# Four shared state buffers instead of three in a hybrid decoder layer, with scratch tiles moved between pools

## The chip, the core and the metric

The kernel runs on one core of a Trainium2 chip. The metric is the device time of one execution in microseconds; for the kernel before, the median of three runs is 1130.1 us (1128.6 to 1131.37). A core has five engines that this text names: PE (TensorE, matmuls), DVE (VectorE), ACT (ScalarE), POOL (GpSimd) and SP (SyncE, which here only issues DMAs). Each runs its own instructions in a fixed order and waits on semaphores where it needs another engine's result.

## The reference, cut to what matters

One inference step of a decoder layer. 512 prompt tokens and 8 samples of 8 new tokens each (576 tokens) go through the same weights. The layer has a mixer (a Mamba-2 SSD with 16 heads and an mLSTM with 4 heads, side by side), a cross-attention and a SwiGLU, each in sandwich norms. The change concerns the recurrences of the samples, which start from a given state and return the new one. For every sample:

```python
# SSD, state h of 16 heads x 64 x 128
y_inter = jnp.einsum('btgn,bgjpn->btgjp', cc, h) * jnp.exp(cum)[..., None]
h_new = h * jnp.exp(cum[:, -1])[..., None, None] + jnp.einsum('bsgj,bsgjp,bsgn->bgjpn', to_end, xc, bc)
...
# mLSTM, state c of 4 heads x 128 x 256, with n beside it
num = jnp.einsum('btsh,bshv->bthv', s, vc) + s_inter[..., None] * jnp.einsum('bthd,bhdv->bthv', qc, c_st)
h = num / jnp.maximum(jnp.abs(den), jnp.exp(-m_t))[..., None]
c_new = scale[..., None, None] * c_st + jnp.einsum('bsh,bshd,bshv->bhdv', w_end, kc, vc)
...
h_ml = _rms(h_ml).reshape(bsz, length, ML_INNER) * g_mlstm_out * jax.nn.sigmoid(og)
mix = jnp.concatenate([y_ssd.astype(x.dtype), h_ml.astype(x.dtype)], axis=-1) @ w_out
```

## The kernel before

Activations lie with features on the 128 partitions and the 576 tokens along the free axis. Every weight matrix comes in tiles of 128 x 1024: SP loads `raw` (two buffers), ACT casts the high part `whi`, DVE subtracts to get the low part `wlo` (or POOL issues an accumulating DMA for half of it), three buffers of each, and PE makes three matmuls for each product (high x high, high x low, low x high). `gemm` (lines 201 to 203) does this for all the large projections; the names `ps_in`, `ps_v`, `ps_o` are its PSUM outputs for the input projection, the values and the output projection.

The mixer is written in this order: start and convolutions; gates; the prompt's SSD (`ssd_prompt`); the samples' SSD; q and k (`qk_tile`), v (`gemm_tok`); the prompt's mLSTM, four heads one after the other; the samples' mLSTM in two halves `hb` of four samples; the z and output-gate projections; and the output projection `ps_o`, whose first half needs `mixs_h` and `mixs_l` (the high and low parts of the SSD's result). The order on the chip is another. In this part the framework's scheduler decides at build time: it models the time and puts each engine's instructions into one fixed order, so that the recurrences lie between the matmuls of the projections. Two things bind it. Buffers of one pool and tag are handed out in the order of the program's text, and a tile that takes a used place waits until everything that read the old one is done. That holds too when a pool is closed and another one takes its place, and for the big slots (`SL`).

The samples' SSD holds one tag `t4` of three buffers of 128 x 1024 fp32: `xdts` and `xes` (used first, with the samples' values), and then the states. Step b (0 to 3) loads two states (L711), reads them on PE (`ps_hs`, L715), multiplies them by their decay on POOL (L722), makes two updates each on PE (`ps_hu`, L725), adds these on DVE (L726) and stores the states from the same buffers (L728).

The samples' mLSTM is alike. Its tag `t4` has three buffers for a state of 128 x 4 x 258: load (L909), four reads on PE into `ps_nh` (L911), a masked copy `km` of the keys on ACT (L914, one buffer), four updates `ps_cu` (L918), each added on DVE (L919, which also scales the old state by `es`), store (L921). At the end of each half stand the norm (`head_norm`, L797 and after), the multiplication L933, a transpose on PE (L936) and a copy by ACT into `qk` (L937). `ps_nh`, `ps_cu` and the transpose share two PSUM buffers (`BP`). `head_norm` squares on ACT into a scratch tile `hn_jk` whose contents nobody reads; only the sums go on. The prompt's heads take it from the pool `mp_`, the samples from the pool `ms`.

After both halves L1011 to L1013 merge the samples' part, and `gn_apply` splits the SSD's result into `mixs_h` (ACT) and `mixs_l` (DVE). `mixs_l` lies in slot 2, where `vt4` (the prompt's values) lay, and `mixs_h` in a right-side pool where the samples' tiles lay. L1006 and L1007 split the mLSTM's part, `mixm_h` and `mixm_l`, for the second half of the output projection.

Of the kernel before, what the change touches and what calls it, by code (L numbers as in the profile page):

```python
# [11 lines left out]
F32 = mybir.dt.float32  # L12
F32R = mybir.dt.float32r
BF16 = mybir.dt.bfloat16
# [5 lines left out]
P = 128  # L20
T = 576
# [95 lines left out]
def build(nc, tc, ctx, I, O):  # L117
# [13 lines left out]
    def SL(slot, name, dt=F32, shape=(P, KT, T)):  # L131

        return big.tile(list(shape), dt, name=name, tag="s%d" % slot, bufs=1)
# [26 lines left out]
    def C16(k):  # L160
        a, b = _c16[k]
        return c16[:, a:b]
# [114 lines left out]
    ml = stv.enter_context(tc.tile_pool(name="ml", bufs=1, reuse_waits="tile"))  # L277

    CT = ml.tile([P, 5, 104], F32, name="CT")
    cumst = ml.tile([80, T], BF16, name="cumst")  # L280
    sxst = ml.tile([68, T], BF16, name="sxst")
    mrow = ml.tile([4, TS], F32, name="mrow")
    ncum = ml.tile([P, 4, 16], F32, name="ncum")
    wend = ml.tile([P, 5, 16], F32, name="wend")
    decp = ml.tile([P, 4, 16], F32, name="decp")
    wendm = ml.tile([P, 5, 4], F32, name="wendm")
    scalem = ml.tile([P, 4, 4], F32, name="scalem")
    expnm = ml.tile([P, 4, 4], F32, name="expnm")
# [4 lines left out]
    U, UL = act(uh), act(ul)  # L293
    rxb = ml.tile([P, T], F32, name="rxb")

    wz = ml.tile([P, 256], BF16, name="wz")
    V.memset(wz, 0.0)
    psw = MP("ps_warm")
    for _ in range(NWARM):
# [29 lines left out]
                mm(ps, wl, ah, start=False, stop=k == KT - 1)  # L329
    with tc.issue_after(uhk.ins), tc.issue_after(ulk.ins):  # L330
        w2 = split_w(I["win"][3], cut=1024)
    st = ExitStack()
    sp = st.enter_context(tc.tile_pool(name="startp", bufs=1, reuse_waits="tile"))
    ssqx = sp.tile([P, 640], F32, name="ssqx")
    G.memset(ssqx[:, T:640], 1.0)

# [43 lines left out]
    bcp = stb.enter_context(tc.tile_pool(name="bcp", bufs=1, reuse_waits="tile"))  # L380
    bc = bcp.tile([P, 4, T], F32, name="bc")
    cdup = bcp.tile([16, 2, TS], F32, name="cdup")


    stgp = ExitStack()
# [178 lines left out]
    def ssd_prompt(g):  # L564
        Bt, Ct = bc[:, g, :], bc[:, 2 + g, :]
        ps = MP("ps_bt")
        for c in range(4):
            TE.transpose(ps[:, c * P:(c + 1) * P], Bt[:, c * P:(c + 1) * P], ident)
        btok = sd.tile([P, 4, P], F32, name="btok", tag="btok")
        A.copy(btok, ps.rearrange("p (c k) -> p c k", c=4))  # L570
        ps = MP("ps_cb")
        for c in range(4):
            mm(ps[:, c * P:(c + 1) * P], Bt[:, c * P:(c + 1) * P], Ct[:, c * P:(c + 1) * P], start=True, stop=True,
               skip_group_check=True)
        cbs = sd.tile([P, 512], F32, name="cbs", tag="cbs")
        A.copy(cbs, ps)
        xdt, hs = [], [None]
        for c in range(4):
            ps = MP("ps_xt")
            for j in range(4):  # L580
                TE.transpose(ps[:, j * P:(j + 1) * P], xs[:, g * 4 + j, c * P:(c + 1) * P], ident)
            xd = sd.tile([P, 8, 64], F32, name="xdt", tag="xdt", bufs=4)
            V.tensor_tensor(xd, ps.rearrange("p (h k) -> p h k", h=8),
                            CT[:, c, 32 + 8 * g:40 + 8 * g].unsqueeze(2).to_broadcast([P, 8, 64]), op=ALU.mult)
            xdt.append(xd)
            xe = sd.tile([P, 8, 64], F32, name="xe", tag="xe", bufs=1)
            G.tensor_tensor(xe, xd, wend[:, c, 8 * g:8 * g + 8].unsqueeze(2).to_broadcast([P, 8, 64]), op=ALU.mult)
            ps = MP("ps_h")
            mm(ps, btok[:, c, :], xe.rearrange("p h k -> p (h k)"), start=True, stop=True)
            h = sd.tile([P, 8, 64], F32, name="hs", tag="hs", bufs=4)  # L590
            p3 = ps.rearrange("p (h k) -> p h k", h=8)
            if c == 0:
                V.tensor_copy(h, p3)
            else:
                G.tensor_tensor(h, hs[c], decp[:, c, 8 * g:8 * g + 8].unsqueeze(2).to_broadcast([P, 8, 64]), op=ALU.mult)
                V.tensor_tensor(h, h, p3, op=ALU.add)
            hs.append(h)
        S.dma_start(O["ssmp"][:, g * 512:(g + 1) * 512], hs[4].rearrange("p h k -> p (h k)"))
        for j in range(4):
            jj = g * 4 + j  # L600
            psi = MP("ps_yi")
            lms = []
            for k in range(2):
                h = 2 * jj + k
                psb = MP("ps_l")
                mm(psb, sel[:80, h:h + 1].to_broadcast([80, P]), cumst[:, 0:TP], start=True, stop=True)
                lm = ml.tile([P, 512], F32, name="lm", tag="tmp", bufs=2)
                for c in range(4):
                    V.scalar_tensor_tensor(lm[:, c * P:(c + 1) * P], psb[:, c * P:(c + 1) * P], ncum[:, c, h:h + 1],
                                           C16("maskp"), op0=ALU.add, op1=ALU.add)  # L610
                A.activation(lm, lm, AF.Exp)
                V.tensor_tensor(lm, lm, cbs, op=ALU.mult)
                lms.append(lm)

            for c in range(4):
                for k in (1, 0):
                    mm(psi[64 * k:64 * k + 64, c * P:(c + 1) * P], xdt[c][:, 2 * j + k, :], lms[k][:, c * P:(c + 1) * P],
                       start=True, stop=True, skip_group_check=True)
            pse = MP("ps_ec")
            for k in range(2):  # L620
                mm(pse[64 * k:64 * k + 64, 0:384], sel[:80, 2 * jj + k:2 * jj + k + 1].to_broadcast([80, 64]),
                   cumst[:, P:TP], start=True, stop=True, skip_group_check=True)
            ec = sd.tile([P, 384], F32, name="ec", tag="ec", bufs=1)
            A.activation(ec, pse[:, 0:384], AF.Exp)
            psn = MP("ps_yn")
            for c in range(1, 4):
                mm(psn[:, (c - 1) * P:c * P], hs[c][:, 2 * j:2 * j + 2, :].rearrange("p h k -> p (h k)"),
                   Ct[:, c * P:(c + 1) * P], start=True, stop=True, skip_group_check=True)
            V.tensor_tensor(ec, ec, psn[:, 0:384], op=ALU.mult)
            V.scalar_tensor_tensor(y[:, jj, 0:TP], xs[:, jj, 0:TP], PAR("dskip", jj), psi, op0=ALU.mult, op1=ALU.add)  # L630
            G.tensor_tensor(y[:, jj, P:TP], y[:, jj, P:TP], ec, op=ALU.add)
# [18 lines left out]

    st2 = ExitStack()
    sd = st2.enter_context(tc.tile_pool(name="ssds", bufs=1, side="right", reuse_waits="tile"))
    masks8 = C16("masks")[:TS, :].unsqueeze(1).to_broadcast([TS, 8, TS])
    xdts = sd.tile([TS, 16, 64], F32, name="xdts", tag="t4", bufs=3)
    xes = sd.tile([TS, 16, 64], F32, name="xes", tag="t4", bufs=3)
    btk = sd.tile([TS, 2, P], F32, name="btk")
    for g in range(2):
        ps = BP("ps_xts")
        for j in range(4):
# [11 lines left out]
    for g in range(2):  # L671
        for hb in range(2):
            dst = cpad[:, g, 4 * hb:4 * hb + 4, :].rearrange("p b t -> p (b t)")
            src = bc[:, 2 + g, TP + 32 * hb:TP + 32 * hb + 32]
            for b in range(4):
                G.tensor_copy(dst[:, b * 40:b * 40 + 8], src[:, b * 8:b * 8 + 8])
    decs = sd.tile([P, 16, NB], F32, name="decs")
    psi = BP("ps_yis")
    for g in range(2):
        psb = BP("ps_ls")  # L680
# [25 lines left out]
    psh = BP("ps_hs")  # L706
    hbs = [stacks(sd, btk.rearrange("p g k -> p (g k)"), xes.rearrange("p h k -> p (h k)"), hb, 2) for hb in range(2)]
    for b in range(4):
        hns = [sd.tile([P, 16, 64], F32, name="h0", tag="t4", bufs=3) for _ in range(2)]
        for hb in range(2):  # L710
            S.dma_start(hns[hb], I["h0"][4 * hb + b])  # L711
        for g in range(2):
# [31 lines left out]
        qk_tile(j)  # L744


    vt4 = SL(2, "vt4", F32, (P, 4, 4, 258))
    vt = [vt4[:, c, :, :] for c in range(4)] + [vts]
    for v_ in vt:
        G.memset(v_[:, :, 256:257], 1.0)  # L750
# [45 lines left out]
    def head_norm(num, ex, n4, pool, name):  # L796

        ss = pool.tile([P, n4], F32, name="hn_ss", tag="hn_ss", bufs=2)
        jk = pool.tile([P, 256], F32, name="hn_jk", tag="hn_jk", bufs=1)
        for c in range(n4):  # L800
            A.activation(jk, num[:, c, 0:256], AF.Square, accum_out=ss[:, c:c + 1])
        d = pool.tile([P, n4], F32, name="hn_d", tag="hn_d", bufs=2)
# [71 lines left out]
    for h in range(4):  # L874
        mm(psb[:, h * TS:(h + 1) * TS], sel[:68, h:h + 1].to_broadcast([68, P]), sxst[:, TP:T], start=h == 0, stop=h == 3,
           skip_group_check=True)
    es = ms.tile([P, 4, TS], F32, name="es")
    A.activation(es, pb3, AF.Exp)
    masks4 = C16("masks")[:TS, :].unsqueeze(1).to_broadcast([TS, 4, TS])
    ds_ = ms.tile([TS, 4, TS], F32, name="ds_")  # L880
# [18 lines left out]
    for hb in range(2):  # L899
# [5 lines left out]
               tile_position=(32 * hb, 32 * h), skip_group_check=True)  # L905
        for b in range(4):
            bb = 4 * hb + b
            c0 = ms.tile([P, 4, 258], F32, name="c0", tag="t4", bufs=3)
            S.dma_start(c0, I["c0"][bb])  # L909
            for h in range(4):  # L910
                mm(psn[32 * h:32 * h + 32, 0:257], qpad[:, h, bb, :], c0[:, h, 0:257], start=False, stop=b == 3,  # L911
                   skip_group_check=True)
            km = ms.tile([96, 512], F32R, name="km", tag="km", bufs=1)
            A.activation(km, kst.bitcast(F32), AF.Copy, scale=C32("bmask")[:96, b:b + 1])  # L914
            cn = c0
            for h in range(4):
                ps = BP("ps_cu")
                mm(ps[:, 0:258], km[:, h * P:(h + 1) * P], vst[:, h * 258:(h + 1) * 258], start=True, stop=True)  # L918
                V.scalar_tensor_tensor(cn[:, h, :], c0[:, h, :], es[:, h, 8 * bb + 7:8 * bb + 8], ps[:, 0:258],  # L919
                                       op0=ALU.mult, op1=ALU.add)  # L920
            S.dma_start(O["cs"][bb], cn)  # L921
# [18 lines left out]


    def tmp():
        return ml.tile([P, 512], F32, name="tmp", tag="tmp", bufs=2)

    def z_evac(j):
        def ev(t0, n, ps):
# [36 lines left out]

    mixm_h = SL(3, "mixm_h", F32R)
    mixm_l = SL(4, "mixm_l", F32R)
    ogs = ml.tile([P, KT, TS], F32, name="ogs")

    def og_evac(j):
        def ev(t0, n, ps):
# [1031 lines left out]
```

## Time and profile before

| | |
|---|---|
| median of 3 runs | 1130.1 us (1128.6 to 1131.37) |
| the profiled execution | 1128.78 us, of which the span from first to last instruction is 1127.0 us |
| busy: PE / DVE / ACT / POOL | 1102.2 / 708.2 / 594.3 / 222.5 us |
| mean granted clock of PE | 0.995 |
| HBM read / written | 158.21 MB / 22.22 MB |

The profile is of one execution. "L715" is line 715 of the kernel before. In an answer about waits the columns are: who waited, on what line, for whom; microseconds in total, how many times, the longest. A row that groups instructions has the count (x32), then the busy time in us and the mean duration in ns, then the idle time of the engine just before them. A row of a timeline has start and duration in us. "SPq" rows are the issue of DMAs. PE's matmuls are pipelined: the duration of one is longer than the distance to the next, so distances are taken from starts.

### The profile page before, as it was taken

To read this page: it belongs to the slowest core of one execution; us is meant where nothing else is said; L and a number is where in the kernel's file an instruction comes from. 1 tells how busy PE (TensorE), PEld (TensorE's weight loads), DVE (VectorE), ACT (ScalarE), POOL (GpSimd) and SP (SyncE) were. 2 spreads that over 40 slices of the span, in tenths; PEclk is the share of its full clock that TensorE was granted. 3 is DMA by queue.
4 is the path that set the end of the run, shared out by engine and by line. 5 is a ranking of instruction groups with operands and counts; after the bars stand their busy time and mean duration, and the time that the engine had idled before them with its cause. 6 is when DMAs were issued, how large, how long until landed. Compare 5 with 4: busy or idle time off the path is not lost.

```text
span 1127.0 us, 21146 instructions
## 1 busy us (share of the span) xinstructions
PE 1102.2 (98%) x8423; PEld 1052.4 (93%) x8423; DVE 708.2 (63%) x1401; ACT 594.3 (53%) x1073; POOL 222.5 (20%) x308
## 2 busy tenths in 40 slices
PE   9999999899999999999999999999999999999996
PEld 8999889798998999999988889999999999999996
DVE  6796874457786675668755456667623765447555
ACT  6877533355563365656544445635435674246543
POOL 1333444322122121100134301101001110011001
PEclk9999999999999999999999999999999999999999
DMA  6685565535574447763477855643535774257532
GB/s 211 166 162 128 130 170 162 157 85 142 145 203 108 126 149 267 266 234 100 156 243 280 279 179 174 234 144 95 168 93 118 168 173 124 94 119 169 123 125 85
DMA packets 57127, 181.82 MB, mean 161 GB/s; under 512 B 6300, under 2 KB 10524, under 8 KB 56516
## 3 DMA queue, kind: packets, MB, share of 16 engines
q1 hardware_dynamic: 41732, 137.99, 37.4%
q0 software_dynamic: 15296, 42.47, 18.0%
q8 instruction: 66, 1.08, 0.4%
q14 instruction: 33, 0.27, 0.1%
HBM read 158.21 MB, written 22.22 MB: 160 GB/s over the span
## 4 chain that ended last, share of the span: by engine, by line
PE 81%; DMA 7%; issue 4%; DVE 4%; ACT 3%; SPq 0%; POOL 0%; DVEq 0%; POOLq 0%; ACTq 0%
PE ps_in L201 5%; PE ps_in L203 5%; PE ps_in L202 5%; PE ps_dn L203 4%; PE ps_dn L201 4%; PE ps_dn L202 4%; PE ps_u L1717 3%; PE ps_u L1716 3%; PE ps_u L1715 3%; PE ps_g L1716 2%; PE ps_g L1715 2%; PE ps_g L1717 2%; PE ps_o L203 2%; PE ps_o L201 2%; PE ps_o L202 2%
## 5 line engine op out<-in xcount | busy, mean ns | idle before, releaser
L181 ACT CAST whi<-raw 128x1024 fp32r<-128x1024 f32 x110 | 114.8, 1045 | 102.9 <-PE ps_dn L202 20.0
L201 PE MATMUL ps_in<-uh,whi 128*128 128x320 f32 (+1 forms) x544 | 166.0, 305 | 0.0
L203 PE MATMUL ps_in<-uh,wlo 128*128 128x320 f32 (+1 forms) x544 | 163.2, 300 | 0.5 <-DVE wlo L188 0.5
L202 PE MATMUL ps_in<-ul,whi 128*128 128x320 f32 (+1 forms) x544 | 162.6, 299 | 0.0
L188 DVE TENSOR_TENSOR wlo<-raw,whi 128x1024 fp32r<-128x1024 f32 (+1 forms) x102 | 102.0, 1000 | 74.0 <-ACT whi L181 69.8
L201 PEld LDWEIGHTS ps_in<-uh,whi 128*128 128x128 f32 x544 | 103.5, 190 | 2.7 <-issue 1.2
L203 PEld LDWEIGHTS ps_in<-uh,wlo 128*128 128x128 f32 x544 | 103.4, 190 | 2.4 <-issue 1.3
L202 PEld LDWEIGHTS ps_in<-ul,whi 128*128 128x128 f32 x544 | 103.6, 190 | 0.7
L203 PE MATMUL ps_dn<-hh,wlo 128*128 128x320 f32 (+1 forms) x280 | 82.4, 296 | 0.6 <-DVE wlo L188 0.6
L202 PE MATMUL ps_dn<-hl,whi 128*128 128x320 f32 (+1 forms) x280 | 82.2, 294 | 0.0
L201 PE MATMUL ps_dn<-hh,whi 128*128 128x320 f32 (+1 forms) x280 | 81.9, 295 | 0.0
L203 PEld LDWEIGHTS ps_dn<-hh,wlo 128*128 128x128 f32 x280 | 52.6, 188 | 0.8 <-DVE wlo L188 0.8
L202 PEld LDWEIGHTS ps_dn<-hl,whi 128*128 128x128 f32 x280 | 52.9, 189 | 0.0
L201 PEld LDWEIGHTS ps_dn<-hh,whi 128*128 128x128 f32 x280 | 52.4, 188 | 0.3 <-ACT hh L192 0.3
L186 POOL DMA_DIRECT2D wlo<-win x32 | 28.4, 887 | 94.8 <-ACT wlo L185 84.4
L1715 PE MATMUL ps_g<-b,whi 128*128 128x288 f32 x144 | 42.5, 295 | 0.2 <-ACT cc L1740 0.2
L1716 PE MATMUL ps_u<-b,whi 128*128 128x288 f32 x144 | 42.5, 295 | 0.0
L1716 PE MATMUL ps_g<-b,whi 128*128 128x288 f32 x144 | 42.5, 295 | 0.0
L1715 PE MATMUL ps_u<-b,whi 128*128 128x288 f32 x144 | 42.5, 295 | 0.0
L201 PE MATMUL ps_o<-mixm_h,whi 128*128 128x256 f32 (+1 forms) x128 | 38.8, 303 | 1.5 <-ACT whi L181 1.5
L201 PE MATMUL ps_xo<-qh,whi 128*128 128x288 f32 x128 | 37.8, 300 | 1.0 <-ACT f_xo L1407 1.0
L202 PE MATMUL ps_o<-mixm_l,whi 128*128 128x256 f32 (+1 forms) x128 | 38.5, 302 | 0.0
(722 smaller groups left out, 3654.5 us busy)
## 6 DMA issues: line engine op xcount, KB each, us to landing
raw<-win SPq DMA_DIRECT2D x35, 512.0 KB, 3.7
raw<-wout SPq DMA_DIRECT2D x17, 512.0 KB, 4.3
kva<-kc SPq DMA_DIRECT2D x16, 512.0 KB, 7.2
kva<-vc SPq DMA_DIRECT2D x16, 512.0 KB, 6.3
raw<-wdown SPq DMA_DIRECT2D x16, 512.0 KB, 3.5
raw<-wxq SPq DMA_DIRECT2D x13, 512.0 KB, 3.7
raw<-wgate SPq DMA_DIRECT2D x13, 512.0 KB, 4.1
raw<-wup SPq DMA_DIRECT2D x13, 512.0 KB, 4.7
```

The lines of the kernel that those rows point to most:

```text
L181: A.copy(hi[:, :n], raw[:, :n])
L186: G.dma_start(lo[:, a:b], src[:, a:b], accum_op=ALU.add)
L188: e.tensor_tensor(lo[:, a:b], raw[:, a:b], hi[:, a:b].bitcast(F32), op=ALU.subtract)
L201: mm(ps, wh, ah, start=i == 0, stop=False)
L202: mm(ps, wh, al, start=False, stop=False)
L203: m = mm(ps, wl, ah, start=False, stop=i == len(tiles) - 1)
L1715: mm(ps, wh, b[0][:, k, :], start=start and k == 0, stop=False, skip_group_check=True)
L1716: mm(ps, wh, b[1][:, k, :], start=False, stop=False, skip_group_check=True)
L1717: m = mm(ps, wl, b[0][:, k, :], start=False, stop=k == 3, skip_group_check=True)
```

## The change

Both tags `t4` get four buffers in place of three. To make room, small tiles move:

- `btk`, `decs` (samples' SSD) and `es` (samples' mLSTM) become parts of one slot-2 tile of 4608 columns, `vt4_`, which also holds `vt4` and is now allocated before the samples' SSD;
- `hn_jk` always comes from the pool `mp_`, for the samples too;
- `cumst`, `ncum`, `wend`, `decp` move from `ml` to `bcp`; `lm` (tag `tmp`) to the SSD's pool, `tmp` and `ogs` to `zp`, `wz` to `startp`, which is opened earlier.

No arithmetic is changed.

```diff
-    cumst = ml.tile([80, T], BF16, name="cumst")
-    ncum = ml.tile([P, 4, 16], F32, name="ncum")
-    wend = ml.tile([P, 5, 16], F32, name="wend")
-    decp = ml.tile([P, 4, 16], F32, name="decp")
...
-    wz = ml.tile([P, 256], BF16, name="wz")
+    st = ExitStack()
+    sp = st.enter_context(tc.tile_pool(name="startp", bufs=1, reuse_waits="tile"))
+    wz = sp.tile([P, 256], BF16, name="wz")
...
+    cumst = bcp.tile([80, T], BF16, name="cumst")
+    ncum = bcp.tile([P, 4, 16], F32, name="ncum")
+    wend = bcp.tile([P, 5, 16], F32, name="wend")
+    decp = bcp.tile([P, 4, 16], F32, name="decp")
...
-                lm = ml.tile([P, 512], F32, name="lm", tag="tmp", bufs=2)
+                lm = sd.tile([P, 512], F32, name="lm", tag="tmp", bufs=2)
...
+    vt4_ = SL(2, "vt4", F32, (P, 4608))
-    xdts = sd.tile([TS, 16, 64], F32, name="xdts", tag="t4", bufs=3)
-    xes = sd.tile([TS, 16, 64], F32, name="xes", tag="t4", bufs=3)
-    btk = sd.tile([TS, 2, P], F32, name="btk")
+    xdts = sd.tile([TS, 16, 64], F32, name="xdts", tag="t4", bufs=4)
+    xes = sd.tile([TS, 16, 64], F32, name="xes", tag="t4", bufs=4)
+    btk = vt4_[:TS, 4128:4384].rearrange("p (g k) -> p g k", g=2)
...
-    decs = sd.tile([P, 16, NB], F32, name="decs")
+    decs = vt4_[:, 4384:4512].rearrange("p (h b) -> p h b", h=16)
...
-        hns = [sd.tile([P, 16, 64], F32, name="h0", tag="t4", bufs=3) for _ in range(2)]
+        hns = [sd.tile([P, 16, 64], F32, name="h0", tag="t4", bufs=4) for _ in range(2)]
...
-    vt4 = SL(2, "vt4", F32, (P, 4, 4, 258))
+    vt4 = vt4_[:, 0:4128].rearrange("p (c h k) -> p c h k", c=4, h=4)
...
-        jk = pool.tile([P, 256], F32, name="hn_jk", tag="hn_jk", bufs=1)
+        jk = mp_.tile([P, 256], F32, name="hn_jk", tag="hn_jk", bufs=1)
...
-    es = ms.tile([P, 4, TS], F32, name="es")
+    es = vt4_[:, 4128:4384].rearrange("p (h t) -> p h t", h=4)
...
-            c0 = ms.tile([P, 4, 258], F32, name="c0", tag="t4", bufs=3)
+            c0 = ms.tile([P, 4, 258], F32, name="c0", tag="t4", bufs=4)
...
-        return ml.tile([P, 512], F32, name="tmp", tag="tmp", bufs=2)
+        return zp.tile([P, 512], F32, name="tmp", tag="tmp", bufs=2)
...
-    ogs = ml.tile([P, KT, TS], F32, name="ogs")
+    ogs = zp.tile([P, KT, TS], F32, name="ogs")
```

More of the change, by code (lines that the diff above doesn't have):

```diff
@@ L331, in build @@
         w2 = split_w(I["win"][3], cut=1024)
-    st = ExitStack()
-    sp = st.enter_context(tc.tile_pool(name="startp", bufs=1, reuse_waits="tile"))
     ssqx = sp.tile([P, 640], F32, name="ssqx")
```

## The prediction, made before the changed kernel ran

> **What bounds the kernel now.** First the page of the profile, its busy times and its chain that ended last.
>
> ```profile
> span 1127.0 us, 21146 instructions
> PE 1102.2 (98%) x8423; PEld 1052.4 (93%) x8423; DVE 708.2 (63%) x1401; ACT 594.3 (53%) x1073; POOL 222.5 (20%) x308
> PE 81%; DMA 7%; issue 4%; DVE 4%; ACT 3%; SPq 0%; POOL 0%; DVEq 0%; POOLq 0%; ACTq 0%
> ```
>
> TensorE (PE) is the bound: its matmuls cover 1102.2 of 1127.0 us, and the diff adds and removes none. In the order of the program as built, the changed kernel has the same instructions on every engine, PE's first 1004 matmuls stand as before, and so does everything after the first few output-projection tiles (`ps_o`). So only PE's idle time can change, and only between about 140 us and there, some 405 us. Second view: what PE waited for, of DMAs in that stretch.
>
> ```profile
> PE ps_hs L715 <- DMA h<-h: 2.6, 1, 2.6
> PE ps_nh L911 <- DMA c<-c: 2.0, 1, 2.0
> PE ps_v L774 <- DMA wlo<-wv: 1.1, 2, 0.8
> ```
>
> Two waits are for states (h, c), one each, 2.6 and 2.0 us. Third view: busy times by stretch, in which the column after the engines is the granted clock.
>
> ```profile
> 204.00:208.00 4.00, 2.93 (x24) 2.09 (x25) 0.69 (x1) 0.80 (x2) 1.76 (x1) 1.00 0.40 162
> 360.00:362.00 2.00, 1.50 (x10) 0.69 (x11) 2.00 (x3) 0.27 (x1) 1.19 (x2) 0.65 0.60 162
> 362.00:364.00 2.00, 2.00 (x11) 2.00 (x10) 2.00 (x7) 0.51 (x2) 0.00 (x0) 0.50 0.89 200
> 364.00:372.00 8.00, 8.00 (x63) 8.00 (x63) 3.91 (x10) 3.07 (x5) 0.00 (x0) 1.00 0.19 72
> ```
>
> After the wait for c the clock was granted at 0.65 and 0.50 for two stretches of 2 us: 2 x 0.35 + 2 x 0.50 = 1.7 us of lost matmul time. After the wait for h it stayed at 1.00. [...]
>
> **The change part by part.** *The fourth state buffer, samples' SSD.* The four steps (b = 0 to 3) each load two states, multiply, add, and store from the same buffer; a load into a used buffer waits for the store. These are the links: PE's last update matmul (L725), issue of the store (L728), issue of the next load (L711), and where PE waited.
>
> ```profile
> 158.05 0.47 PE L725 MATMUL ps_hu<-stb,bm 96*128 96x512 f32 x1
> 159.58 0.34 SPq L728 DMA_DIRECT2D o_ssms<-h  x1
> 162.24 0.33 SPq L711 DMA_DIRECT2D h<-h  x1
> 169.66 0.48 PE L725 MATMUL ps_hu<-stb,bm 96*128 96x512 f32 x1
> 171.23 0.34 SPq L728 DMA_DIRECT2D o_ssms<-h  x1
> 176.35 0.33 SPq L711 DMA_DIRECT2D h<-h  x1
> 189.94 1.27 SPq L176 DMA_DIRECT2D raw<-wv  x2
> 190.17 0.39 PE L725 MATMUL ps_hu<-stb,bm 96*128 96x512 f32 x1
> 191.52 0.34 SPq L728 DMA_DIRECT2D o_ssms<-h  x1
> 200.83 0.33 SPq L711 DMA_DIRECT2D h<-h  x1
> 205.07 1.07 PE L715 MATMUL ps_hs<-h,cpad 128*32 128x512 f32 x8 [2.58 <-DMA h<-h]
> DMA to landing us min/median/max: 3.6/4.2/6.4
> ```
>
> With 4.2 us for a landing, the chain from matmul to landed state took 162.24 + 4.2 - 158.05 = 8.4, 176.35 + 4.2 - 169.66 = 10.9, and 14.9 us. The new buffer lets step 1 load early, but the scheduler spends it: as built, step 1's reads stand directly behind step 0's first update, and steps 2 and 3 stand only some 9.6 and 9.9 us of PE work behind the update that their buffer waits for (an estimate, from the matmuls between; before, the one that stalled had 205.07 - 2.58 - 190.17 = 12.3). Such a chain against 9.7 us gives a wait of 0, 1.2 or 5.2 us. The long one had two weight loads issued just ahead of its store (189.94). Two waits of the two shorter kinds give 1.2 together on the mean, two of all three kinds 4.3, against 2.6 saved: -1.4 or +1.7. I take 0 for the net; the ends are -2.6 (no wait) and +7.8 (two long ones). SP's queue meets the same: a load that waits for a store holds the weight loads behind it. The 1.1 us for `wlo` stay: POOL's two multiplies now stand ahead of one weight transfer, where POOL had several us idle.
>
> *The fourth buffer, samples' mLSTM.* The first half's four states load at once, and the second half's four long before their use, so the wait for c and its clock go: -2.0 - 1.7 = -3.7 us. A fourth load in the first burst delays the weight load behind it; cover is the two raw buffers. The second half's stores, on the other hand, come late and stand in SP's queue ahead of the sixth and later output weights; cover: five of these are issued before or between them, and PE needs no sixth for many us after `ps_o` starts.
>
> *The moved tiles.* `wz`, `cumst`, `ncum`, `wend`, `decp`, `lm`, `tmp`, `ogs`, `btk`, `decs`: no instruction more, nothing earlier on PE; `cumst`'s memset goes to a later place of an idle POOL. Zero, the cover being that bc's pool had to be released before the z tiles anyway (`ssqg` lay in its place). `es` now lies in `vt4`'s slot, which `mixs_l` takes next, so `mixs_l` waits for the last samples' update; by the order below it comes behind it in any case.
>
> *The one that matters: `hn_jk`.* This scratch (one buffer) was the samples' own, in `mls`. Now it lies in `mp_`, where the four prompt heads use it; buffers are handed out in program order, and the samples' code stands behind all four heads. So the samples' first norm now waits for the fourth head's squares: in ACT's built order `hn_jk<-nums` directly follows the last `hn_jk<-num`. The first half's transpose (L936) drops behind the last prompt head. The PSUM buffers are handed out in that order too, so the whole second half follows it: 16 reads of states, 16 updates `ps_cu` with 16 additions on DVE, the norm, the transpose. Thirteen of the `ps_cu` stand in one block behind the last `ps_in`, and then come L928, L936 and the first `ps_o`. Before, they were spread between input-projection matmuls. The durations:
>
> ```profile
> L919 DVE SCALAR_TENSOR_TENSOR c<-c,es,ps_cu 128x258 f32<-128x258 f32 x32 | 14.8, 478 | 2.8 <-PE ps_cu L918 2.7
> L1007 DVE SCALAR_TENSOR_TENSOR mixm_l<-qk,ghalf,mixm_h 128x512 fp32r<-128x512 f32 x8 | 5.5, 744 | 0.0
> L914 ACT ACTIVATE km<-sta,c 96x512 fp32r<-96x512 f32 x8 | 5.8, 723 | 5.1 <-PE ps_cu L918 4.9 <-DVE sta L645 0.2
> L188 DVE TENSOR_TENSOR wlo<-raw,whi 128x1024 fp32r<-128x1024 f32 x5 | 6.1, 1222 | 2.0 <-ACT whi L181 2.0
> L994 DVE SCALAR_TENSOR_TENSOR qk<-tmp,qk 128x256 f32<-128x256 f32 x16 | 6.7, 426 | 1.0 <-ACT tmp L992 1.0
> L991 DVE TENSOR_TENSOR tmp<-ps_in,rxb 128x320 f32<-128x320 f32 x8 | 3.9, 491 | 2.8 <-PE ps_in L203 2.7
> ```
>
> And the tail as it ran before, by the timelines of DVE, ACT and PE:
>
> ```profile
> 382.12 0.87 DVE L919 SCALAR_TENSOR_TENSOR c<-c,es,ps_cu 128x258 f32<-128x258 f32 x2
> 394.29 0.15 DVE L812 TENSOR_SCALAR hn_v<-hn_v 128x1 f32<-128x1 f32 x1
> 395.42 0.15 DVE L814 TENSOR_TENSOR hn_a<-hn_y 128x1 f32<-128x1 f32 x1
> 396.19 0.35 DVE L933 TENSOR_SCALAR hns<-nums,hn_a 128x256 f32<-128x256 f32 x1
> 399.19 0.38 PE L936 MATMUL ps_hts<-c,hns 128*128 128x128 f32 x2
> 399.61 0.37 ACT L937 COPY qk<-ps_hts 128x256 f32<-128x256 f32 x1
> 399.88 2.40 ACT L192 CAST mixs_h<-xs 128x576 fp32r<-128x576 f32 x4
> 400.08 0.42 DVE L1011 SCALAR_TENSOR_TENSOR ogs<-ogs,qk 128x256 f32<-128x256 f32 x1
> 400.59 0.76 DVE L193 TENSOR_TENSOR mixs_l<-xs,mixs_h 128x576 fp32r<-128x576 f32 x1
> 408.14 4.72 DVE L1007 SCALAR_TENSOR_TENSOR mixm_l<-qk,ghalf,mixm_h 128x512 fp32r<-128x512 f32 x7
> 404.21 0.31 PE L203 MATMUL ps_in<-uh,wlo 128*128 128x320 f32 x1
> 404.36 0.28 PE L201 MATMUL ps_o<-mixs_h,whi 128*128 128x256 f32 x1
> ```
>
> Before, 5 us of `ps_in` matmuls lay between the last transpose (399.19) and `ps_o` (404.36) and hid the splits of `mixs`. In the built order nothing lies there. From the second half's first `ps_cu`, DVE has in order: 16 L919 at 0.43 (two in 0.87) = 7.0; 8 L1007 at 0.67 (seven in 4.72) = 5.4, whose `mixm_l` nobody needs yet; one L188, 1.1; two L991 and two L994, 1.6; the copy and a small one, 0.5: 15.6 us. Waits inside: some 1.3 us at the second `ps_cu`, which stands behind 24 `ps_in` (0.15 us each, 404.21 to 404.36), and about 1.7 where `km` (one buffer) must be remade on ACT after a step's last `ps_cu` (0.72 and the hand-overs): estimate 3, so 18.6. Then the tail: L928 and its exponential 0.4, five small ones 0.9, POOL's power 1.1 (394.29 to 395.42), 0.8 to L933, 0.5 to the transpose, 0.4 to ACT's copy, 0.5 to L1011, two of these and the first `mixs_l` 1.5: 6.1. With 0.3 to start: 25.0 us. PE's own work over that stretch is 29 `ps_in` (4.4), 15 `ps_cu` (about 0.15 each, 2.3) and the small ones 0.8: 7.5. PE stands for 25.0 - 7.5 = 17.5 us. Bounds: without the inner waits 14.5; with L919 and L1007 at their full 0.478 and 0.744 us and every `km` exposed, 22. Behind it `ps_o` runs on `mixs_l` splits at 0.67 us a piece with L1012 between: +0.7; and the clock falls as behind the wait for c, +1.7 (0 to 3.4, two such stretches).
>
> Sum on the profiled execution, 1128.8 us (span 1127.0): 17.5 + 0.7 + 1.7 - 3.7 + 0 = +16.2, 1145.0. The median of the runs, 1130.1, is 1.3 higher: 1146.3, forecast 1146.
>
> **The rivals.** A, faster: the state waits go and nothing replaces them. [...] It gives 2.6 + 2.0 + 1.7 saved, 1123.8. For it: both waits are in PE's list. It decides if under 7.5 us pass from the second half's first `ps_cu` to the first `mixs_l`; against it, DVE's ordered 15.6 us alone are twice that. 3%.
>
> B, the changed order costs about what the waits gave: a tail stall of 6 us (the second half starting well before PE gets through its `ps_in`), 1130.1 + 6 - 6.3, about 1130. Against it: the second half's matmuls stand behind the transpose. 3%.
>
> C, the tail stall half as long, since DVE's other work finishes before: 9 + 2.4 - 3.7, 1138. 12%.
>
> D, worse: the state chains meet slow stores in both steps (+7.8) and the clock falls there too (+1.7), or a weight load stuck behind a waiting store adds that: 1146 + 9.5, about 1156. 12%.
>
> **How the numbers follow.** My forecast gets 70%: 1146, with its bounds 14.5 to 22 and -2.6 to +4 around it. The range reaches down to C and up nearly to D: 1138 to 1155. A measurement can tell about 0.3% (3.4 us). Faster is A, 3%; same is B, 3%; slower the rest, 94%.
>
> **What would show it.** In the new profile: no wait of PE for c; a stretch around 380 to 405 us where PE idles some 15 us while DVE is full of L919 and L1007, with thirteen `ps_cu` one after the other; `hn_jk<-nums` behind the prompt's squares on ACT; `ps_o` released by `mixs_l`; a granted clock of 0.50 just behind. In the SSD steps waits of `ps_hs` for h of 0 to 5 us. Wrong if `ps_o` starts within 5 us of its place before, or if PE's idle time grew somewhere else.

## The result: slower, 1145.6 us

| | kernel before | changed kernel |
|---|---|---|
| median | 1129.9 us (1128.6 to 1131.4, 4 runs) | 1145.6 us (1143.1 to 1147.8, 4 runs) |
| profiled execution (span) | 1128.8 us (1127.0) | 1145.0 us (1143.2) |

The ratio is 1.0148, with a 95% interval of 1.0122 to 1.0174 (the quotient of the two medians, 1.0139, lies inside it). The forecast was 1146.0, in a range of 1138 to 1155. The medians shift by some 2 us from one series to another, so each kernel below has its ratio to the kernel before in the same series.

The page of the changed kernel, busy times and the chain that ended last:

```profile
span 1143.2 us, 21133 instructions
PE 1109.3 (97%) x8423; PEld 1054.8 (92%) x8423; DVE 708.7 (62%) x1401; ACT 595.2 (52%) x1073; POOL 221.3 (19%) x308
PE 81%; DVE 5%; DMA 5%; issue 4%; ACT 3%; POOL 1%; SPq 0%; DVEq 0%; POOLq 0%; ACTq 0%
```

The span grew by 16.2 us and PE's busy time by 7.1, with the same 8423 matmuls: part of the work ran at a lower clock (on the mean 0.987 after 0.995), as the rows below show. In the chain DMA lost two points and DVE won one. The list of what PE waited for names the place:

```profile
PE ps_cu L919 <- ACT km L915: 5.5, 3, 3.3
PE ps_o L201 <- ACT whi L181: 3.5, 2, 2.1
PE ps_hts L937 <- DVE hns L934: 3.0, 1, 3.0
PE ps_cu L919 <- DVE c L920: 1.9, 4, 0.8
PE ps_o L201 <- ACT mixs_h L192: 1.0, 1, 1.0
```

(Line numbers in that part of the new kernel are one higher.) The waits for h and for c are gone from the list. New are the waits of `ps_cu` for `km` and for the addition on DVE, that of the transpose for `hns`, and the one for `mixs_h`: 5.5 + 3.0 + 1.9 + 1.0 = 11.4 us, all between 398 and 418 us. The busy times by stretch there (PE, weight loads, DVE, ACT, POOL, then the granted clock):

```profile
400.00:404.00 4.00, 1.75 (x4) 1.07 (x4) 4.00 (x8) 4.00 (x7) 0.00 (x0) 0.54 0.75 263
404.00:408.00 4.00, 1.58 (x5) 0.87 (x4) 4.00 (x10) 1.97 (x4) 0.24 (x1) 0.50 0.25 103
...
412.00:416.00 4.00, 0.97 (x4) 0.55 (x4) 1.89 (x11) 0.17 (x1) 2.37 (x6) 0.50 0.42 147
416.00:420.00 4.00, 2.97 (x12) 2.72 (x12) 3.50 (x7) 3.90 (x8) 0.00 (x0) 0.50 0.96 379
420.00:424.00 4.00, 4.00 (x31) 4.00 (x30) 3.82 (x6) 1.73 (x4) 0.00 (x0) 0.90 0.19 68
```

For eight us DVE has no gap, and PE starts eight matmuls (one that runs over 404 us is counted in both rows); ACT is full in the first four. Then follows the tail, in which four engines (PE, ACT, DVE, POOL) hand one small thing to each other (PE 0.97 us of 4). The clock is at half for some 20 us, from about 400 us on (0.54 from 400 to 404, 0.50 from 404 to 420). Two timelines of the same stretch, ACT and PE:

```profile
383.04 0.42 ACT L802 ACTIVATE hn_jk<-num 128x256 f32<-128x256 f32 x1 [2.09 <-DVE num L850]
383.58 0.42 ACT L802 ACTIVATE hn_jk<-nums 128x256 f32<-128x256 f32 x1
...
399.26 1.95 ACT L1007 ACTIVATE mixm_h<-qk,ghalf 128x512 fp32r<-128x512 f32 x3
401.11 0.71 ACT L915 ACTIVATE km<-sta,c 96x512 fp32r<-96x512 f32 x1
401.72 2.55 ACT L1007 ACTIVATE mixm_h<-qk,ghalf 128x512 fp32r<-128x512 f32 x4
```

```profile
392.47 0.38 PE L919 MATMUL ps_cu<-stb,km 96*128 96x258 f32 x1
401.87 0.80 PE L919 MATMUL ps_cu<-stb,km 96*128 96x258 f32 x2 [3.33 <-ACT km L915]
410.61 0.97 PE L919 MATMUL ps_cu<-stb,km 96*128 96x258 f32 x2 [0.36 <-DVE c L920]
417.10 1.06 PE L201 MATMUL ps_o<-mixs_h,whi 128*128 128x256 f32 x3 [1.03 <-ACT mixs_h L192]
417.99 0.58 PE L202 MATMUL ps_o<-mixs_l,whi 128*128 128x256 f32 x1
```

The samples' squares (`hn_jk<-nums`) come directly after the fourth prompt head's (`hn_jk<-num`), as the shared scratch orders it. So the second half's sixteen updates start at 392.47 us, and the last thirteen stand in one block behind `ps_in`. In the kernel before, the last of all 32 updates had started by 385.5 us:

```profile
L918 PE MATMUL ps_cu<-stb,km x32: 279/286/471, 276.7 to 385.5; 96*128 96x258 f32 x32
```

From the second half's first `ps_cu` (392.47) to the first `mixs_l` matmul (417.99) pass 25.5 us. PE is idle for 11.6 us of it. The longest wait, 3.33 us for `km`, is one that ACT caused: it had three splits of `mixm_h` in front of the first copy, and four more in front of the next.

### The profile page after: what moved, and what is told of

It is laid out like the page before. It is cut to its first block, busy times and chain, and to the rows that moved or that the text cites. A ratio compares the mean times of both kernels' runs of the same rounds, so it can differ in the third digit from the quotient of the medians.

```text
span 1143.2 us, 21133 instructions
## 1 busy us (share of the span) xinstructions
PE 1109.3 (97%) x8423; PEld 1054.8 (92%) x8423; DVE 708.7 (62%) x1401; ACT 595.2 (52%) x1073; POOL 221.3 (19%) x308
## 3 DMA queue, kind: packets, MB, share of 16 engines
q0 software_dynamic: 15296, 42.47, 17.8%
## 4 chain that ended last, share of the span: by engine, by line
PE 81%; DVE 5%; DMA 5%; issue 4%; ACT 3%; POOL 1%; SPq 0%; DVEq 0%; POOLq 0%; ACTq 0%
PE ps_in L201 5%; PE ps_in L202 5%; PE ps_in L203 5%; PE ps_dn L203 4%; PE ps_dn L201 4%; PE ps_dn L202 4%; PE ps_u L1718 3%; PE ps_u L1717 3%; PE ps_u L1716 3%; PE ps_g L1716 2%; PE ps_g L1717 2%; PE ps_g L1718 2%; PE ps_o L201 2%; PE ps_o L203 2%; PE ps_o L202 2%
## 5 line engine op out<-in xcount | busy, mean ns | idle before, releaser
L188 DVE TENSOR_TENSOR wlo<-raw,whi 128x1024 fp32r<-128x1024 f32 (+1 forms) x102 | 104.5, 1024 | 86.1 <-ACT whi L181 85.9
L201 PE MATMUL ps_o<-mixs_h,whi 128*128 128x256 f32 (+1 forms) x128 | 38.3, 303 | 1.0 <-ACT mixs_h L192 1.0
```

The costliest lines, as they stand in the source:

```text
L188: e.tensor_tensor(lo[:, a:b], raw[:, a:b], hi[:, a:b].bitcast(F32), op=ALU.subtract)
L201: mm(ps, wh, ah, start=i == 0, stop=False)
```

## The experiments

**The scratch alone, out of the change.** The samples' scratch goes into the slot of their own `hns` tile, which is written only after the squares are used. No space is needed for that.

```diff
-        jk = mp_.tile([P, 256], F32, name="hn_jk", tag="hn_jk", bufs=1)
+        jk = pool.tile([P, 256], F32, name="hn_jk", tag="hn_jk" if n4 > 1 else "hns", bufs=1)
```

> The changed kernel, but the samples' scratch for squares lies in the slot of their own hns tile again (no space more), not in the one that the prompt heads use. Theory (the shared scratch holds the samples' second half back): the sixteen ps_cu spread between ps_in matmuls again, the stall of PE ahead of ps_o (12.7 us of lateness at the first ps_o) and its half clock go, and the gain of the state buffers is left: before minus 3 to 4 us, about 1126 (1124 to 1129). Rival 1 (es in the slot of vt, or another moved tile, holds the output projection back): no change, 1143 to 1147. Rival 2 (the fourth buffers themselves order PE's work badly): 1140 or more.

Measured: 1130.1 us, ratio 1.0017 (0.9997 to 1.0037). The stall is gone: no `ps_cu` is left in PE's list of waits. All moved tiles and the fourth buffers are still there, so neither `es` in the slot of `vt4` nor another moved tile nor the buffers make it by themselves. But the gain that was expected beside that (1126) isn't there. Its waits of PE, and rows of PE and ACT behind the start of the output projection:

```profile
PE ps_o L201 <- ACT whi L181: 3.0, 2, 2.1
PE ps_o L201 <- ACT f_mix L1111: 2.2, 1, 2.2
PE ps_ss L1462 <- DVE ssqxo L1538: 1.9, 1, 1.9
```

```profile
397.50 0.28 PE L201 MATMUL ps_o<-mixs_h,whi 128*128 128x256 f32 x1
403.56 0.41 PE L201 MATMUL ps_o<-mixs_h,whi 128*128 128x320 f32 x1 [2.18 <-ACT f_mix L1111]
```

```profile
398.51 3.78 ACT L1007 ACTIVATE mixm_h<-qk,ghalf 128x512 fp32r<-128x512 f32 x6
402.20 1.04 ACT L868 COPY qk<-ps_ht 128x512 f32<-128x512 f32 x2
403.14 0.37 ACT L1111 COPY f_mix<-ps_o 128x256 f32<-128x256 f32 x1
```

`ps_o` starts at 397.50, 6.9 us before its place in the kernel before (404.36). Then its second group of matmuls waits 2.18 us for the first group's copy, `f_mix`, which stands on ACT behind six splits and two copies of the last prompt head. A matmul that starts at 417.44 in the kernel before starts at 415.44 here, so 2.0 of the 6.9 us are left by then: the wait took 2.2, the granted clock (0.57 from 404 to 408) 4 x 0.43 = 1.7, and the last head's eight transposes, which now stand behind the start of `ps_o` (399.16), the remaining 1.0. The other two waits in the list took 1.5 and 1.9 us more than in the kernel before, and with them the lead is gone.

**The scratch alone, put into the kernel before.** Only that line changes (`pool.tile` to `mp_.tile`).

> The kernel before with one edit: the samples' squares go to the scratch of the prompt heads. Three buffers, es and all small tiles stay. Theory: this edit alone makes the stall; as built, fourteen ps_cu stand in one block ahead of ps_o: plus 17.5 of stall, 2.4 behind it, and minus 3.7 since the samples' late second half no longer waits for c: about 1146 (1142 to 1150). Rivals (moved tiles, buffers): 1130, no change.

Measured: 1154.0 us, ratio 1.0215 (1.0165 to 1.0266). One edit, which changes nothing that is computed, costs at least as much as the whole change (the two intervals just overlap). Its waits of PE:

```profile
PE ps_cu L918 <- ACT km L914: 6.1, 3, 4.4
PE ps_cu L918 <- DVE c L919: 3.3, 5, 1.6
...
PE ps_hs L715 <- DMA h<-h: 2.9, 1, 2.9
PE ps_nh L911 <- DMA c<-c: 2.3, 1, 2.3
```

The direction is as expected, but the time lies above the expected range (1142 to 1150): the size was taken 8 us too low. The -3.7 was wrong: I let the wait for c go with the second half's later place, and it is there. The waits of `ps_cu` are 9.4 us in all, where the changed kernel has 7.4, and the wait for h stays too. The rest of the 8 us was not traced.

**Three buffers in both places, all else as changed.**

> The changed kernel with three buffers in both places again, all tiles moved and the scratch shared. Theory: the stall is there without the fourth buffers: 1143 to 1149, with the wait for h (2.6 us, clock at full speed) back in PE's list. Rival 2 (the fourth buffers order the work badly): back to about 1130.

Measured: 1151.5 us, ratio 1.0208 (1.0166 to 1.0249), 0.6% above the changed kernel and above the expected range (1143 to 1149). So the stall needs no fourth buffer, and rival 2 falls. Its list has the same waits of `ps_cu` as before_shared (6.1 and 3.3 us, the longest 4.4). The wait for h in the list, and the one for c on PE's timeline:

```profile
PE ps_hs L716 <- DMA h<-h: 2.6, 1, 2.6
```

```profile
410.69 1.09 PE L912 MATMUL ps_nh<-c,qpad 128*32 128x257 f32 x8 [2.14 <-DMA c<-c]
```

The wait for c now lies inside the block of `ps_cu`, at half clock (0.50 from 408 to 412). So with the shared scratch the fourth buffers do seem to pay, some 6 us, though the two intervals just overlap: two waits for states (2.6 and 2.1 us), and a shorter block (thirteen `ps_cu` in place of fourteen, with 2.0 us less of waits).

**The splits of `mixm`, held behind the tail.** PE's order up to the start of `ps_o` is the same; ACT and DVE make the eight splits later.

```diff
-    for j in range(8):
-        hm = qk[:, 4 * (j % 2) + j // 2, 0:TP]
+    with tc.issue_after(hts_.ins):
+        for j in range(8):
+            hm = qk[:, 4 * (j % 2) + j // 2, 0:TP]
...
```

(`hts_` is ACT's copy of the samples' last transpose.)

> The changed kernel with the eight prompt splits of mixm (ACT and DVE) held behind the copy of the samples' last transpose; PE's order is the same. Theory (the tail's length is the sum of what DVE and ACT have in order, 5.5 us of it mixm_l and 5 us of ACT's mixm_h ahead of the km): the stretch from the second half's first ps_cu to the first mixs_l matmul shrinks from 25.5 to 20 or 21 us, the time to about 1140.5 (1139 to 1142.5). Rival (the chain ps_cu, addition, next PSUM buffer sets the pace and the splits only fill its gaps): 25 us, 1144 to 1147.

Measured: 1138.8 us, ratio 1.0100 (1.0066 to 1.0134), just below the expected range (1139 to 1142.5); the profiled span is 3.9 us below that of the changed kernel. The wait for `km` in the list, and PE's timeline:

```profile
PE ps_cu L919 <- ACT km L915: 3.2, 3, 1.5
```

```profile
391.90 0.38 PE L919 MATMUL ps_cu<-stb,km 96*128 96x258 f32 x1
402.72 0.80 PE L919 MATMUL ps_cu<-stb,km 96*128 96x258 f32 x2 [0.87 <-ACT km L915]
405.72 0.80 PE L919 MATMUL ps_cu<-stb,km 96*128 96x258 f32 x2 [0.87 <-ACT km L915]
406.88 0.98 PE L919 MATMUL ps_cu<-stb,km 96*128 96x258 f32 x2 [0.36 <-DVE c L920]
413.37 1.06 PE L201 MATMUL ps_o<-mixs_h,whi 128*128 128x256 f32 x3 [1.03 <-ACT mixs_h L192]
414.26 0.58 PE L202 MATMUL ps_o<-mixs_l,whi 128*128 128x256 f32 x1
```

The stretch is 414.26 - 391.90 = 22.4 us, 3.2 shorter, where 4.5 to 5.5 were expected. DVE's 5.5 us of splits were thus a little over half on the path. That the medians lie 6.8 us apart (0.5% by the ratios), more than the stretch or the two profiles show, stays unexplained. With them gone, the chain sets the pace: a step of `km`, four `ps_cu` and four additions takes 3.0 us (402.72 to 405.72), though the four additions are some 1.8 us of it (0.88 us for two, in the changed kernel). Theory and rival both hold a part. From the last pair of `ps_cu` to `ps_o` it is 413.37 - 406.88 = 6.5 us, as in the changed kernel (417.10 - 410.61). In neither kernel does DVE have other work in that tail, so these two do not show what other work there would cost.

**Two buffers of the shared scratch** (and three for c, to make room).

> The changed kernel with two buffers of the shared scratch in place of one, and three buffers for c to make room for it. The samples' first norm then waits for the third prompt head only; as built, six of the second half's sixteen ps_cu stand between ps_in matmuls again and ten stand in one block ahead of ps_o. Theory (the stall is what DVE and ACT have in order from there on): the second half's block is six additions and two km shorter than in three_bufs, so about 6 to 9 us faster than three_bufs (1151.5): 1142 to 1146. Rival (the stall hangs on one wait at the end, whatever stands in the block): as three_bufs, 1149 or more. Other rival (one buffer more frees it all): 1130 to 1133.

Measured: 1145.9 us, ratio 1.0160 (1.0132 to 1.0188). It lies where the theory put it (1142 to 1146), but not for that reason alone. It has four buffers for h, and its list has no wait for h or c (2.6 and 2.1 us in three_bufs); a kernel that differs from it in the scratch alone (one buffer, four for h, three for c) was not run. The waits of `ps_cu` fell only from 9.4 to 7.8 us:

```profile
PE ps_cu L919 <- ACT km L915: 5.8, 2, 4.9
PE ps_cu L919 <- DVE c L920: 2.0, 2, 1.7
```

Ten `ps_cu` stand in the block, as expected, where three_bufs has fourteen; that saved little of the waits, as one wait for `km` alone takes 4.9 us. What the run shows is that a buffer more does not free the second half.

**With a scratch of its own: which buffers pay?** Three kernels as own_scratch, with three buffers again for both, for c, and for h.

> Own scratch (in the slot of hns) and three buffers for h and for c: of the change only the moved tiles are left. Theory 1 (the gain of the fourth buffers is real up to the output projection and is lost behind it: a wait of PE for the first copy of ps_o, 2.2 us, and the weights' transfers some 480 us, which stood at the same absolute time in the kernel before and in own_scratch): both state waits (2.6 and 2.0 us) are back, the last prompt head still runs late, about 1132 (1129 to 1135). Theory 2 (the moved tiles cost some 3 to 4 us by themselves): 1134 or more, and own_scratch without them would be 1126. Rival (nothing of it matters): 1128 to 1130, as before.

> Own scratch, four buffers for h, three for c. Theory 1: no wait for h in PE's list, the wait for c (2.0 us, with its half clock, 1.7) stays unless PE's order moves it; lateness at the first ps_o between own_3_3 and own_scratch; time 1129 to 1132, since the transfers behind give nothing of it back. If the buffers' gains simply add: own_3_3 minus 2.6.

> Own scratch, three buffers for h, four for c. Theory 1: the wait for h stays (2.6 us), none for c; 1129 to 1132. If the gains simply add: own_3_3 minus 3.7.

Measured: own_3_3 1131.6 us, ratio 1.0019 (0.9999 to 1.0039); own_h4 1130.6, 1.0024 (1.0005 to 1.0043); own_c4 1130.0, 1.0016 (0.9992 to 1.0040). With own_scratch (1.0017) that is four kernels within 0.1%: the number of buffers makes no difference that can be measured, where one interval spans some 0.4%. The wait for h of own_3_3 and, below it, of own_c4:

```profile
PE ps_hs L716 <- DMA h<-h: 0.4, 1, 0.4
```

```profile
PE ps_hs L716 <- DMA h<-h: 2.7, 1, 2.7
```

With three buffers for c nothing waits for c any more, which I had not expected. The groups of the reads, of the kernel before and of own_3_3, with the first and the last start:

```profile
L911 PE MATMUL ps_nh<-c,qpad x64: 380/380/635, 274.1 to 360.9; 128*32 128x257 f32 x64
```

```profile
L912 PE MATMUL ps_nh<-c,qpad x64: 380/380/405, 257.5 to 347.3; 128*32 128x257 f32 x64
```

With three buffers in both kernels, the moved tiles let the samples run earlier, from 257.5 us in place of 274.1; with the shared scratch it is the same (260.6 in three_bufs, 278.0 in before_shared). That this is why the wait went was not tested by itself. The wait for h is 0.4 us in one profile and 2.7 in another with the same number of buffers. All four lose 2.2 us or more at the wait for `f_mix`.

**The copy of `f_mix`.** own_scratch and own_3_3 with two edits: the splits of `mixm` behind the copy of the last prompt head's transpose, and the first output tile's copies on DVE.

```diff
+    with tc.issue_after(htp_.ins):
...
-              lambda t0, n, ps: evs.append(A.copy(f[:, j, t0:t0 + n], ps)), "ps_o1")
+              lambda t0, n, ps: evs.append((A.copy if j else V.tensor_copy)(f[:, j, t0:t0 + n], ps)), "ps_o1")
```

> own_scratch (four buffers, own scratch) with two more edits: the eight splits of mixm are held behind the copy of the last prompt head's transpose, and the first output tile's copies (f_mix) are made by DVE in place of ACT, where they stood behind six of those splits. Theory (in own_scratch 3.7 us or more are gained ahead of the output projection, 2 to 3 of them are lost at the wait for the first f_mix, 1.7 at the weights some 480 us): the f_mix wait of 2.2 us and the half clock behind it go; if PE is the bound behind it, before minus 3 to 5: 1124 to 1127. Rival (the weights' transfers pace the projection's end, at the same absolute time, some 475 us, whatever PE gains ahead of it): the wait for whi some 480 us grows by what the f_mix wait gave, 1128 to 1131, as before.

> The same two edits on own_3_3 (three buffers each). If the fourth buffers' gain is real (the waits for h and c, 2.6 + 2.0 + 1.7 us): 3 to 6 us slower than own_dve_copy. If the weights' transfers pace the projection's end: within 1.5 us of own_dve_copy and of the kernel before.

Measured: own_dve_copy 1126.9 us, ratio 0.9975 (0.9949 to 1.0001); own_33_dve_copy 1127.1, 0.9971 (0.9949 to 0.9993). Both lie about 0.3% below the kernel before, which only the second interval separates from no change, and below the kernels that they were made from. The three buffers do as well as the four, so the expected 3 to 6 us between them are not there; but own_33_dve_copy is not within 1.5 us of the kernel before either. The row at which own_scratch waited 2.18 us, and the two at the weights, of own_dve_copy:

```profile
402.47 0.42 PE L201 MATMUL ps_o<-mixs_h,whi 128*128 128x320 f32 x1 [0.51 <-DVE tmp L992]
478.30 0.41 PE L201 MATMUL ps_o<-mixm_h,whi 128*128 128x320 f32 x1 [1.93 <-ACT whi L181]
479.91 0.63 PE L201 MATMUL ps_o<-mixm_h,whi 128*128 128x320 f32 x1 [1.06 <-ACT whi L181]
```

The wait at that matmul is down to 0.51 us. Of the lead that PE has after that, own_dve_copy spends a part at the weights (1.93 + 1.06 = 3.0 us; own_33_dve_copy waits only 1.7 there), where the kernel before waits 1.5 us in all (its list, and the second of the two on its timeline):

```profile
PE ps_o L201 <- ACT whi L181: 1.5, 2, 1.0
```

```profile
483.09 0.41 PE L201 MATMUL ps_o<-mixm_h,whi 128*128 128x320 f32 x1 [1.01 <-ACT whi L181]
```

But the second of these matmuls in own_dve_copy comes 3.2 us earlier (479.91 against 483.09): the transfers do not stand at a fixed time, and the rival in that form falls. Which of the two edits brings how much was not separated.

## Why the prediction was right, step by step

**PE is the bound, and only its idle time before `ps_o` can change.** Right about the place, only half right about the idle time: PE's busy time grew too, by 7.1 of the 16.2 us, since the matmuls between the waits ran at half clock (0.50 to 0.54 in the rows from 400 to 420 us), one or two at a time. From the first matmul of L568 to `ps_o`, PE was idle for 13.3 us in place of 6.8. The first `ps_o` came 417.10 - 404.36 = 12.7 us late, the end 16.2. But 1.2 us of it stood before the place of the change: the first matmul of L568 started at 102.19 after 100.96.

```profile
102.19 0.60 PE L568 MATMUL ps_bt<-c,bc 128*128 128x128 f32 x4
```

Other builds had there from -0.4 to +0.7; so it is most likely this execution's, not the edit's.

**The buffer for h: 0.** The 2.6 us are gone and the waits of 0 to 5 us in steps 2 and 3 were 0: the result lies at the good end (-2.6) and not at the 0 that went into the sum. own_3_3 and own_c4 (0.4 and 2.7 us) show that what this buffer is worth depends on the execution and the order.

**The buffer for c: -3.7.** The wait went, as predicted. That the buffer was its cause is less sure: with the moved tiles and three buffers (own_3_3) it went as well, and with three buffers and the shared scratch it came back in another place.

**The moved tiles: 0.** Right for the time (own_3_3: 1.0019, 0.9999 to 1.0039), wrong for the order: with three buffers for c they start the samples earlier, and in all kernels with their own scratch the last prompt head's transposes stand behind the start of `ps_o`, where their copies add to the wait for `f_mix`. How much of the latter comes from the scratch's new slot was not separated.

**The shared scratch: a stall of 17.5 (14.5 to 22).** This is the cause, shown from both sides: taken out of the changed kernel 1.0148 becomes 1.0017, put into the kernel before 1 becomes 1.0215. The stretch was forecast as 25.0 us and was 25.5. The stall itself comes to some 17.8: 12.7 late at `ps_o`, less 1.2 from the start, and what went elsewhere, 2.6 for h and the 3.7 of c with its clock. The sum's composition was only half right. It added up DVE's work (15.6) and small waits (3), but ACT's splits ahead of `km` were left out (waits of 5.5 us in place of 1.7), and when the splits of both engines went, 3.2 us went, not 5.5. And it had PE idle for 17.5 us and at work for 7.5: PE was idle for 11.6 and busy for 13.9, as the clock was at half from 400 us on and some matmuls had not been counted (14 reads `ps_nh` at 392.78). The tail, from DVE's last addition (412.11) to the first `mixs_l` matmul (417.99), was forecast as 6.1 us and was 5.9.

**Behind it +0.7 and +1.7.** The matmul at 417.44 in the kernel before is at 432.04, 14.6 us late: 1.9 more than the first `ps_o`, against 2.4. The clock alone gives that (0.50 from 417.10 to 420 and 0.90 to 424: 1.45 + 0.4), and the list has no wait for `mixs_l`, so the 0.7 for its pace was not seen. Not forecast were 2.0 us at the weights, where the list has 3.5 us of waits for `whi` after 1.5; why is not shown. So that the sum of +16.2 was met to the tenth is luck: the 2.6 us of h, which the sum did not take off, and 0.5 too much behind `ps_o` stand against 1.2 at the start and 2.0 at the weights. That the main term, the stall, came out within half a us is luck in part too, as its composition shows.

**The signs.** The block of thirteen `ps_cu`, the order of the squares and the missing wait for c came as named. Three did not: PE idled 11.6 us there and not some 15, the clock fell inside the stretch (from 400 us) and not just behind it, and `ps_o` waited for `mixs_h` (1.0 us), not for `mixs_l`. And PE's idle time did grow elsewhere, by the 2.0 us at the weights, which the forecast had named as a sign against it.

**The rivals.** A fell with its condition: 25.5 us, not under 7.5, passed before `mixs_l`. B, which needed a stall of 6 us, fell with it. C (DVE's other work already done) did not happen here; mixm_late, which takes that work out, has 1138.8 us, near the 1138 of C. D's slow chains were not seen.

## What to carry to other kernels

Before a scratch tile is shared to save a kilobyte per partition, ask who used that buffer last in the order of the program: a tile whose contents nobody reads can still put one stage behind another. Here that cost 2% in the kernel before, while fourth buffers gave nothing measurable once the scratch was the samples' own. Look for a slot that the same stage owns and doesn't need yet (`hns`); with it the stall was gone. And a wait removed from the list of waits is only a lead: follow the same matmul in both traces to the end of the stage, since the next late thing (here a copy behind splits, then weights) may take it back.

## What the runs showed of the hardware

In mixm_late the granted clock went from 1.00 to 0.63 and 0.50 although no wait of PE up to there was over 1.5 us (PE busy, weight loads, DVE, ACT, POOL, clock):

```profile
398.00:400.00 2.00, 0.51 (x2) 0.30 (x2) 2.00 (x4) 1.77 (x3) 0.17 (x1) 1.00 0.16 64
400.00:402.00 2.00, 0.98 (x2) 0.58 (x2) 1.72 (x6) 0.06 (x1) 0.14 (x1) 0.63 0.88 278
402.00:404.00 2.00, 0.93 (x3) 0.63 (x3) 1.03 (x3) 0.66 (x1) 0.00 (x0) 0.50 0.90 345
```

PE was busy for 2.4 of these 6 us, and for 0.51 of the first two. In the changed kernel dense matmuls start at 417.10; the clock is 0.50 from 416 to 420, 0.90 from 420 to 424 and 1.00 from 424 to 428. For the same 8423 matmuls PE is busy for 1103.7 us in own_scratch, 1109.3 in the changed kernel and 1113.4 in before_shared; how much of that lies on the path was not separated.

After a single wait of some 2 us the clock fell in one execution and not in another: behind the 2.2 us for `f_mix` it was 0.57 in own_scratch (404 to 408) and 1.00 in own_h4 (404 to 412). What decides it is not shown by these runs.
